# Attention with a bias on one core: three landing tiles for V, a smaller V ring, two spare E tiles, and three moves of V placed later

## The chip, the cores and the metric

The kernel runs on one core of one Trainium2 chip. The metric is the device time in microseconds (us) of one execution; lower is better. The same kernel is run several times, and the median counts.

## The reference: what is computed

```python
def setup_inputs():
    batch, n_heads, seq_len, head_dim = 4, 8, 1024, 64
    # q, k, v: (4, 8, 1024, 64) float32; bias: (1, 1, 1024, 1024) float32; all randn * 0.1

def reference(q, k, v, bias):
    scale = 1.0 / np.sqrt(head_dim)
    scores = scale * np.matmul(q, k.transpose(0, 1, 3, 2)) + bias
    scores_max = np.max(scores, axis=-1, keepdims=True)
    attn = np.exp(scores - scores_max) / (np.sum(np.exp(scores - scores_max), axis=-1, keepdims=True) + 1e-8)
    return np.matmul(attn, v).astype(np.float32)
```

So 32 heads of softmax attention, each of 1024 queries by 1024 keys, with one bias for all heads.

## The kernel before

**Tiling.** The 32 heads are taken as 16 pairs (pr), and the pairs in two groups of 7 and 9. One unit of work, a *slot*, is one chunk of 128 queries of one head against all 1024 keys: 256 slots. Scores live in three score places (`pl`, two PSUM banks each), and a slot belongs to place 0, 1 or 2. Scores are kept in a place from head to head: a fill adds to a place the difference between the next head's scores and the last one's (the arrays ke and qe hold this head's and the negated former head's halves), so the bias is put in only where a chunk starts in a place (`start`, L241), and every other fill is 8 matmuls of 128 x 128 (L244).

**A slot's way.** TensorE fills its place (L244). ScalarE takes the exponential into a bf16 tile E (`exp`, L258). TensorE multiplies E with V (`av`, L312), 8 matmuls into one of the 7 units of a PSUM bank `po`; a column of ones in V gives the row sum. When a bank has 7 units (or 6), VectorE evacuates it (`evac`: reciprocal L320, multiply L322 into `ob`), and stores go out on SP's queue; for the last two banks of the kernel they go out on ScalarE's queue (`close`, L679). There is no subtraction of the maximum.

**Slots on VectorE.** Twenty slots, all of place 2, take their exponential on VectorE instead (`d_steps`): a first step from the place into `dy` (L275), then df, dt, df, dt, de (L280 to L295). The first step sets place 2 free. Up to three such slots are open at a time, two of them in their later steps.

**Loads.** K, Q, V and bias come by DMA from GpSimd's queue (POOL), which turns float32 into bf16 on the way. POOL issues in order. From pair 7 on each load first waits, by a tiny copy (`tick`, L467), for the landing of the load but one before. K and Q are transposed by TensorE into `px` and copied out by VectorE (ko L199, qo L201), and further copies (ke, qe) are made by VectorE, or from pair 7 on by DMAs on SP's queue (L538). The late query chunks of pairs 0 and 1 are loads of their own (`qrest`). The loads stand early on POOL in this order: k1, q1, v0, k2, q2, k3, q3, v1, k4, q4, v2, k5, q5, v3, k6, q6, v4, v5, bias chunk 3, qrest of pairs 0 and 1, bias chunk 4, v6, bias chunks 5 to 7.

**V.** A pair's V lands in a tile of the pool `vland` (2 tiles), and a copy on VectorE (`move_v`, L492) moves it into the ring `vall` of VR = 24 heads, that is 12 pairs, where `av` reads it. So V of pair p may be moved only when all slots of pair p - 12 have been multiplied, and loaded only when V of pair p - 2 has left its landing tile.

**The order of the work** is fixed when the program is built. A planner inside the kernel (the loop at its end) keeps a clock for each engine with costs written by hand, and in each round lets the engine that can start first take its next piece: `pe_pick` for TensorE, `dve_pick` for VectorE (by ready time, then a priority), the oldest filled slot for ScalarE, the earliest ready DMA for SP. POOL gets a load when `next_v` or `load` issues it. On the chip every engine runs its list in order, and waits only where data or a buffer is missing. Whether a slot goes to VectorE is decided at its fill by `may_d` and an estimate of VectorE's `backlog`. The planner lets ScalarE write an E tile only when the slot NE = 13 exps earlier has been multiplied; the pool `ep` has as many tiles.

Of the kernel before, what the change touches and what calls it, by code (L numbers as in the profile page):

```python
# [16 lines left out]
def kernel(  # L17
# [31 lines left out]
    RING = 9  # L49
    LANDS = 5  # L50
    NE = 13
    C0 = 3

    consts = ctx.enter_context(tc.tile_pool(name="consts", bufs=1))
    land = ctx.enter_context(tc.tile_pool(name="land", bufs=LANDS))
    vland = ctx.enter_context(tc.tile_pool(name="vland", bufs=2))
    kq = ctx.enter_context(tc.tile_pool(name="kq", bufs=RING))
    ep = ctx.enter_context(tc.tile_pool(name="ep", bufs=NE))
    op = ctx.enter_context(tc.tile_pool(name="op", bufs=2))
    dp = ctx.enter_context(tc.tile_pool(name="dp", bufs=2))  # L60
    dy = ctx.enter_context(tc.tile_pool(name="dy", bufs=3))
# [15 lines left out]
    zeros = ep.tile([P, NCH, P], BF, name="E")[:, :4].rearrange("p c q -> p (c q)")  # L77
    braw = consts.tile([P, NCH, S], BF)

    VR = 24  # L80
    vall = consts.tile([P, VR, NCH, D1], BF)

    b0f = dp.tile([P, S], F32, name="df")
# [5 lines left out]
    slots = []  # L89
# [20 lines left out]
    NS = len(slots)  # L110
# [10 lines left out]
        at_place[x[0]] = s  # L121

    dslots = set()
    may_d = [x[0] == 2 and 36 < s < NS - 18 and not any(y[3] for y in slots[s:s + 4]) for s, x in enumerate(slots)]

    raws, lands, arrs = {}, {}, {}

# [205 lines left out]
    with tc.manual_schedule():  # L335
# [65 lines left out]
        v_at, vland_at = {}, {0: 13000}  # L401
        t_dma = 15900
        DUE = (64, 82, 94, 106, 117, 126, 134, 142, 150)
        t_pe, t_act, t_dve, t_pool = 9300.0, 9900.0, 9600.0, 9000
# [23 lines left out]
        dav = []  # L428
        dve_q = []
# [6 lines left out]
        free_lands, loads, loads_v = set(), list(range(EARLY, NP)), []  # L436
        sp_q, t_sp = [], T0
        AHEAD, SLACK = 60, 300
        DEP = 115
        ROOM = 5000  # L440
        MARGIN = 0
        WINDOW = 4

# [37 lines left out]
        def next_v(t):  # L481

            while loads_v and not any(x[2] // 2 == loads_v[0] - VR // 2 and y not in av_done for y, x in enumerate(slots)):
                if loads_v[0] - 2 not in v_at:
                    break
                p = loads_v.pop(0)
                vland_at[p] = issue(t, 1600, LATE, load_v, p)
                move_v(p)

        def move_v(pr):  # L490
            def run(t2):
                nc.vector.tensor_copy(vall[:, 2 * pr % VR:2 * pr % VR + 2, :, :D], lands[pr, "v"][:])  # L492
                v_at[pr] = t2 + 480 + L_DVE
                next_v(v_at[pr])
            dve_q.append((vland_at[pr], 0.3, 480, run))


        def early(kind, pr):
# [76 lines left out]
        def pe_cands():  # L575

            out = []
            for x in range(3):
                if not queue[x] or queue[x][0] > next_fill + WINDOW:
                    continue  # L580
                s = queue[x][0]
                r = fill_ready(s)
                if r is not None and (before[s] is None or before[s] in used):
                    cost = FILL + BIAS * bool(slots[s][3] and s > 1)

                    def do(t, s=s, x=x, cost=cost):
                        nonlocal next_fill
                        fill(s)
                        filled[s] = t + cost + L_PE
                        queue[x].pop(0)  # L590
                        next_fill = min([y[0] for y in queue.values() if y], default=NS)
                        if may_d[s] and backlog(t) < ROOM and len(open_d) < 3:
                            dslots.add(s)
                            avq.remove(s)
                            start_d(s)
                        else:
                            acts.append(s)
                    out.append((max(t_pe, r), cost, do, 0, s))
# [15 lines left out]
            if todo:  # L614
                r, group = min(todo)
# [4 lines left out]
                else:  # L620
                    f, tag = min((x_free[y], y) for y in x_free)
                    r = max(r, f)
# [19 lines left out]
            if pieces:  # L642
                pr, which, c0, n = pieces[0]
# [3 lines left out]
                if ((pr, which, c0) in raw_at and next_fill >= need - AHEAD and (ring < 0 or last_slot[ring] < next_fill)  # L647
                        and (lag < 4 or need - next_fill < 8)):
                    f, tag = min((x_free[y], y) for y in x_free)
                    r = max(f, raw_at[pr, which, c0])  # L650
# [40 lines left out]

        chains, d_wait, open_d = [], [], set()

        def backlog(t):
            x = max(0, t_dve - t) + sum(y[2] for y in dve_q if y[0] < t + 3000 and y[1] < 3)
            return x + sum(sum(y[0] for y in c) for c in chains) / 2 + sum(sum(y[0] for y in c[1:]) for r, s, c in d_wait) / 2

        def start_d(s):
            steps = d_steps(s)
            open_d.add(s)  # L700

            def first(t):
                steps[0][1]()
                used[s] = t + steps[0][0] + L_DVE
                d_wait.append((t + steps[0][0] + DEP, s, steps))
                next_chain(t)
            dve_q.append((filled[s], 0.5, steps[0][0], first))
# [46 lines left out]
            return min(ok + fills, key=lambda x: (x[0], x[3])) if ok + fills else None  # L754

        def dve_pick():
            can = [x for x in dve_q if x[1] < 4 or len(dav) < 2]
            if not can:
                return None
            best = min(can, key=lambda x: (max(x[0], t_dve), x[1]))  # L760
            start = max(best[0], t_dve)

            if best[1] >= 3:
                soon = [x for x in dve_q if x[1] < 3 and x[0] < start + 350]
                if soon:
                    best = min(soon, key=lambda x: (x[0], x[1]))
            return best
# [4 lines left out]
        while next_fill < NS or next_act < len(acts) or avq or dav or dve_q or sp_q:  # L772
            c = []
            if next_act < len(acts):

                s = min(x for x in acts[next_act:] if filled[x] <= max(t_act, filled[acts[next_act]]))
                acts.remove(s)
                acts.insert(next_act, s)
                if next_act < NE or acts[next_act - NE] in av_done:
                    r = max(t_act, filled[s], av_done[acts[next_act - NE]] if next_act >= NE else 0)  # L780
# [62 lines left out]
```

## Time and profile before

| what | value |
|---|---|
| median of 3 runs | 235.19 us (233.59 to 235.63) |
| the profiled execution | 235.16 us; its span, from the first to the last instruction, 233.4 us |
| granted TensorE clock | 0.997 |
| TensorE matmuls, busy | 222.3 us (95% of the span) |
| ScalarE, busy | 221.1 us (95%) |
| VectorE, busy | 201.5 us (86%) |
| GpSimd, busy | 63.4 us (27%) |
| exps on ScalarE (L258) | 237, 218.0 us busy, 1089 ns each |
| first steps on VectorE (L275) | 20, 1220 ns each |
| loads of V | 16 of 256 KB, median 6.1 us from issue to landing |

The profile shows one execution. Busy time of an engine is the union of its instructions, which may overlap. "Idle before, releaser" in a row is the time in which the engine had nothing running, and what ended it. Lines are named by their number in the kernel before (L312), tiles by their names in it (`po<-vall,E` writes po and reads vall and E).

### The profile page before, as it was taken

How to read it: one execution, taken by the hardware profiler on the slowest of the kernel's cores; microseconds unless marked ns; L12 is line 12 of the kernel's file. 1: busy time of each engine (PE TensorE's matmuls, PEld its weight loads, DVE VectorE, ACT ScalarE, POOL GpSimd, SP SyncE). 2: the span in 40 equal slices, each digit the busy share in tenths (PEclk: the TensorE clock that was granted, in tenths of full speed). 3: DMA queues.
4: the chain of work that ended last, by engine and by line, in shares of the span. 5: the costliest groups of instructions: out<-in, count | busy, mean ns of one | idle time of the engine just before them, and what ended most of it. 6: DMA issues, size and time to landing. Idle time of an engine off the chain costs nothing. (4 is left out here: it accounts for less than half of the span.)

```text
span 233.4 us, 10703 instructions
## 1 busy us (share of the span) xinstructions
PE 222.3 (95%) x4671; PEld 209.3 (90%) x4671; DVE 201.5 (86%) x296; ACT 221.1 (95%) x241; POOL 63.4 (27%) x99
## 2 busy tenths in 40 slices
PE   7989999899999999999999997999999999999992
PEld 2869999798999999999999997999999999999982
DVE  2576677599999998999999869999998999999972
ACT  3799999988999999999999998999999999999993
POOL 8943135055446555245352310000000000000000
PEclk9999999999999999999999999999999999999998
DMA  6999979959999899999999992111111111221212
GB/s 206 206 205 215 224 166 158 229 121 150 120 191 137 131 159 183 204 196 157 197 163 201 204 194 68 44 42 39 44 37 42 45 42 42 65 59 42 66 48 56
DMA packets 55646, 29.75 MB, mean 127 GB/s; under 512 B 31472, under 2 KB 51952, under 8 KB 55600
## 3 DMA queue, kind: packets, MB, share of 16 engines
q0 software_dynamic: 30336, 14.06, 48.7%
q1 hardware_dynamic: 24832, 14.40, 22.6%
q8 instruction: 36, 0.59, 1.1%
q10 hardware_dynamic: 432, 0.62, 0.8%
q14 instruction: 10, 0.08, 0.1%
HBM read 29.36 MB, written 8.39 MB: 162 GB/s over the span
## 5 line engine op out<-in xcount | busy, mean ns | idle before, releaser
L258 ACT ACTIVATE E<-pl 128x1024 bf16<-128x1024 f32 (+1 forms) x237 | 218.0, 1089 | 4.3 <-PE pl L244 3.9
L312 PE MATMUL po<-vall,E 128*128 128x65 bf16 x1888 | 93.6, 194 | 0.9 <-ACT E L258 0.9
L312 PEld LDWEIGHTS <-E 128*128 128x128 bf16 x1888 | 78.1, 98 | 1.9 <-ACT E L258 1.2
L244 PE MATMUL pl<-qo,ko 128*128 128x128 bf16 x1024 | 77.3, 219 | 1.7 <-DVE dy L275 1.1
L244 PEld LDWEIGHTS <-ko 128*128 128x128 bf16 x1160 | 69.2, 98 | 4.5 <-issue 1.5
L244 PE MATMUL pl<-qe,ke 128*128 128x128 bf16 x888 | 66.8, 219 | 1.9 <-DVE qe L212 0.5
L244 PEld LDWEIGHTS <-ke 128*128 128x128 bf16 x888 | 53.2, 98 | 5.0 <-issue 1.3
L275 DVE TENSOR_SCALAR dy<-pl 128x1024 int32<-128x1024 f32 x20 | 24.4, 1220 | 2.1 <-PE pl L244 1.4
L322 DVE TENSOR_TENSOR ob<-po,rs 128x448 f32<-128x448 f32 (+2 forms) x39 | 23.2, 594 | 1.9 <-DVE rs L320 0.5
L295 DVE SCALAR_TENSOR_TENSOR de<-dy,dt 128x1024 uint16<-128x1024 int32 x20 | 24.4, 1218 | 0.0
L290 DVE SCALAR_TENSOR_TENSOR dt<-df,dt 128x1024 f32<-128x1024 f32 x20 | 24.4, 1218 | 0.0
L284 DVE SCALAR_TENSOR_TENSOR dt<-df 128x1024 f32<-128x1024 f32 x20 | 24.3, 1217 | 0.0
L287 DVE SCALAR_TENSOR_TENSOR df<-dt,df 128x1024 f32<-128x1024 f32 x20 | 24.3, 1216 | 0.0
L199 DVE COPY ko<-px 128x1024 bf16<-128x1024 bf16 (+1 forms) x16 | 10.7, 671 | 6.9 <-PE px L191 6.3
L165 POOL DMA_DIRECT2D v<-in_v_dram x16 | 11.4, 712 | 18.3 <-DVE vall L492 16.0
L138 POOL DMA_DIRECT2D q<-in_q_dram x18 | 16.0, 890 | 1.3 <-DMA out_dram<-ob 0.5
L201 DVE TENSOR_SCALAR qo<-px,sgn 128x1024 bf16<-128x1024 bf16 (+2 forms) x18 | 12.4, 688 | 4.4 <-PE px L191 3.6
L280 DVE TENSOR_SCALAR df<-dy 128x1024 f32<-128x1024 uint16 x20 | 13.8, 690 | 0.0
L241 PE MATMUL pl<-ident,braw 128*128 128x128 bf16 x136 | 11.5, 228 | 0.1
L145 POOL DMA_DIRECT2D k<-in_k_dram x15 | 11.0, 734 | 2.2 <-PE pl L244 1.0
L320 DVE RECIPROCAL rs<-po 128x7 f32<-128x7 f32 (+3 forms) x40 | 7.8, 195 | 4.4 <-PE po L312 4.0
L467 POOL COPY tick<-q 1x1 bf16<-1x1 bf16 x9 | 3.8, 421 | 24.7 <-DMA q<-in_q_dram 24.7
(54 smaller groups left out, 129.5 us busy)
## 6 DMA issues: line engine op xcount, KB each, us to landing
v<-in_v_dram POOLq DMA_DIRECT2D x16, 256.0 KB, 6.1
k<-in_k_dram POOLq DMA_DIRECT2D x15, 256.0 KB, 5.6
out_dram<-ob SPq DMA_DIRECT2D x32, 96.0 KB, 3.6
out_dram<-ob SPq DMA_DIRECT2D x45, 64.0 KB, 3.2
ke<-ko SPq DMA_DIRECT2D x22, 128.0 KB, 4.9
q<-in_q_dram POOLq DMA_DIRECT2D x18, 128.0 KB, 4.8
qe<-q SPq DMA_DIRECT2D x17, 128.0 KB, 4.9
out_dram<-ob SPq DMA_DIRECT2D x67, 32.0 KB, 1.8
```

The costliest lines, as they stand in the source:

```text
L138: nc.gpsimd.dma_start(out=t[:, :, y, :], in_=(qf, kf)[x][pr][:, y].rearrange("p (c d) -> p c d", d=D))
L201: nc.vector.tensor_scalar(t["qo"][:, cs, :], px[:], sgn[:], None, op0=ALU.mult)
L244: nc.tensor.matmul(to, kk[:, kc, :], qq[:, c, :], start=False, stop=True, skip_group_check=True)
L258: nc.scalar.activation(e[:, i:i + n].rearrange("p b x -> p (b x)"), places[slots[s][0]][:, i:i + n].rearrange("p b x -> p (b x)"), ACTF.Ex ...
L275: w.tensor_scalar(t["y"][:], places[slots[s][0]].rearrange("p b x -> p (b x)"), scale * LOG2E * 65536.0, 127.0 * 65536.0, op0=ALU.mult, op ...
L280: w.tensor_scalar(t["f"][:], t["lo"], G / 65536.0, None, op0=ALU.mult)
L284: w.scalar_tensor_tensor(t["t"][:], t["f"][:], -G, t["f"][:], op0=ALU.add, op1=ALU.mult)
L287: w.scalar_tensor_tensor(t["f"][:], t["t"][:], Q, t["f"][:], op0=ALU.mult, op1=ALU.add)
L290: w.scalar_tensor_tensor(t["t"][:], t["f"][:], V, t["t"][:], op0=ALU.add, op1=ALU.mult)
L295: w.scalar_tensor_tensor(etile[s].bitcast(U16).rearrange("p c q -> p (c q)"), t["y"][:], 1.0 / 512.0, t["t"][:], op0=ALU.mult, op1=ALU.add)
L312: nc.tensor.matmul(po[:, j + i, :], etile[s][:, kc, :], vall[:, slots[s][2] % VR, kc, :], start=j + i + kc == 0, stop=kc == NCH - 1, skip_ ...
L322: nc.vector.tensor_tensor(ob[:, :n, :], po[:, :n, :D], rs[:, :n, :].to_broadcast([P, n, D]), op=ALU.mult)
```

## The change

- `vland` has 3 tiles instead of 2 (VL), and a load of V waits for the move of the V three pairs before instead of two.
- The ring `vall` holds 18 heads (9 pairs) instead of 24: V of pair p waits for the slots of pair p - 9.
- `ep` has 15 tiles; the planner goes on planning with 13.
- The slots that go to VectorE are given by a list, PLAN, in place of the estimate. The list holds the twenty slots that the estimate chose before.
- The limit of three open slots on VectorE is now kept when VectorE picks a first step, and no longer at the fill.
- The planner counts V of pairs 13 to 15 as landed 2.5 us later than it did, so their moves come later in VectorE's order.

Since the planner places everything, the order of the three parts follows: on POOL, V of pair 8 goes out ahead of K of pair 11, and V of pairs 9 to 15 all behind Q of pair 15 (before, V of pairs 8, 9 and 10 stood among the loads of K and Q). From there on VectorE's and TensorE's lists differ in places, with the same number of instructions of each kind but for the sizes of some evacuations. At the end, ScalarE's queue has five stores instead of two: the last bank but one holds six units instead of two.

```diff
--- before.py
+++ after.py
@@ -49,13 +49,16 @@
     RING = 9
     LANDS = 5
     NE = 13
+    VL = 3
+
+    SPARE = 2
     C0 = 3
 
     consts = ctx.enter_context(tc.tile_pool(name="consts", bufs=1))
     land = ctx.enter_context(tc.tile_pool(name="land", bufs=LANDS))
-    vland = ctx.enter_context(tc.tile_pool(name="vland", bufs=2))
+    vland = ctx.enter_context(tc.tile_pool(name="vland", bufs=VL))
     kq = ctx.enter_context(tc.tile_pool(name="kq", bufs=RING))
-    ep = ctx.enter_context(tc.tile_pool(name="ep", bufs=NE))
+    ep = ctx.enter_context(tc.tile_pool(name="ep", bufs=NE + SPARE))
     op = ctx.enter_context(tc.tile_pool(name="op", bufs=2))
     dp = ctx.enter_context(tc.tile_pool(name="dp", bufs=2))
     dy = ctx.enter_context(tc.tile_pool(name="dy", bufs=3))
@@ -77,7 +80,7 @@
     zeros = ep.tile([P, NCH, P], BF, name="E")[:, :4].rearrange("p c q -> p (c q)")
     braw = consts.tile([P, NCH, S], BF)
 
-    VR = 24
+    VR = 18
     vall = consts.tile([P, VR, NCH, D1], BF)
 
     b0f = dp.tile([P, S], F32, name="df")
@@ -121,9 +124,8 @@
         at_place[x[0]] = s
 
 
-
     dslots = set()
-    may_d = [x[0] == 2 and 36 < s < NS - 18 and not any(y[3] for y in slots[s:s + 4]) for s, x in enumerate(slots)]
+    PLAN = (38, 47, 50, 59, 75, 78, 96, 108, 117, 129, 150, 159, 171, 177, 189, 195, 207, 216, 225, 234)
 
     raws, lands, arrs = {}, {}, {}
 
@@ -437,7 +439,6 @@
         sp_q, t_sp = [], T0
         AHEAD, SLACK = 60, 300
         DEP = 115
-        ROOM = 5000
         MARGIN = 0
         WINDOW = 4
 
@@ -481,7 +482,7 @@
         def next_v(t):
 
             while loads_v and not any(x[2] // 2 == loads_v[0] - VR // 2 and y not in av_done for y, x in enumerate(slots)):
-                if loads_v[0] - 2 not in v_at:
+                if loads_v[0] - VL not in v_at:
                     break
                 p = loads_v.pop(0)
                 vland_at[p] = issue(t, 1600, LATE, load_v, p)
@@ -492,7 +493,7 @@
                 nc.vector.tensor_copy(vall[:, 2 * pr % VR:2 * pr % VR + 2, :, :D], lands[pr, "v"][:])
                 v_at[pr] = t2 + 480 + L_DVE
                 next_v(v_at[pr])
-            dve_q.append((vland_at[pr], 0.3, 480, run))
+            dve_q.append((vland_at[pr] + 2500 * (pr > 12), 0.3, 480, run))
 
 
         def early(kind, pr):
@@ -589,7 +590,7 @@
                         filled[s] = t + cost + L_PE
                         queue[x].pop(0)
                         next_fill = min([y[0] for y in queue.values() if y], default=NS)
-                        if may_d[s] and backlog(t) < ROOM and len(open_d) < 3:
+                        if s in PLAN:
                             dslots.add(s)
                             avq.remove(s)
                             start_d(s)
@@ -691,15 +692,10 @@
 
         chains, d_wait, open_d = [], [], set()
 
-        def backlog(t):
-            x = max(0, t_dve - t) + sum(y[2] for y in dve_q if y[0] < t + 3000 and y[1] < 3)
-            return x + sum(sum(y[0] for y in c) for c in chains) / 2 + sum(sum(y[0] for y in c[1:]) for r, s, c in d_wait) / 2
-
         def start_d(s):
             steps = d_steps(s)
-            open_d.add(s)
-
             def first(t):
+                open_d.add(s)
                 steps[0][1]()
                 used[s] = t + steps[0][0] + L_DVE
                 d_wait.append((t + steps[0][0] + DEP, s, steps))
@@ -754,14 +750,15 @@
             return min(ok + fills, key=lambda x: (x[0], x[3])) if ok + fills else None
 
         def dve_pick():
-            can = [x for x in dve_q if x[1] < 4 or len(dav) < 2]
+
+            can = [x for x in dve_q if (x[1] < 4 or len(dav) < 2) and (x[1] != 0.5 or len(open_d) < 3)]
             if not can:
                 return None
             best = min(can, key=lambda x: (max(x[0], t_dve), x[1]))
             start = max(best[0], t_dve)
 
             if best[1] >= 3:
-                soon = [x for x in dve_q if x[1] < 3 and x[0] < start + 350]
+                soon = [x for x in can if x[1] < 3 and x[0] < start + 350]
                 if soon:
                     best = min(soon, key=lambda x: (x[0], x[1]))
             return best
```

## The prediction

> **What bounds the kernel now.** I read the page first: ScalarE (ACT) and TensorE (PE) are busy 95% of the span, VectorE (DVE) 86%, GpSimd (POOL) 27%. One group holds ACT: 237 exps, 1089 ns each. They overlap: the last unbroken run of them is 94 in 86.31 us, so the pitch is (86.31 - 1.09) / 93 = 0.916 us, and the 237 alone need 217 of the 233.4 us. What can still be won is where that pitch breaks. The windows of the span show where:
>
> ```profile
> 40.00:50.00 10.00, 9.22 (x196) 8.81 (x194) 6.91 (x14) 9.10 (x11) 0.63 (x1) 1.00 1.02 203
> 50.00:60.00 10.00, 9.59 (x206) 9.11 (x202) 9.86 (x13) 9.41 (x11) 6.92 (x11) 1.00 1.01 119
> 140.00:150.00 10.00, 8.70 (x193) 8.33 (x190) 9.84 (x15) 9.13 (x11) 0.00 (x0) 1.00 0.23 64
> ```
>
> The columns after the length are PE, its weight loads, DVE, ACT, POOL, clock, DMA share and GB/s. ACT stands at 9.9 to 10.0 nearly everywhere else, at full clock. ACT's timeline names the holes (those under 0.2 us are not marked; windows of 2 us show idle of 0.10 in 42 to 44 and 0.13 in 44 to 46):
>
> ```profile
> 47.53 1.02 ACT L258 ACTIVATE E<-pl 128x1024 bf16<-128x1024 f32 x1 [0.26 <-PE pl L244]
> 55.28 17.52 ACT L258 ACTIVATE E<-pl 128x1024 bf16<-128x1024 f32 x19 [0.59 <-PE pl L244]
> 73.14 69.23 ACT L258 ACTIVATE E<-pl 128x1024 bf16<-128x1024 f32 x75 [0.34 <-PE pl L244]
> 143.24 86.31 ACT L258 ACTIVATE E<-pl 128x1024 bf16<-128x1024 f32 x94 [0.87 <-PE pl L244]
> ```
>
> An idle time of g costs ACT g + (1.09 - 0.92) = g + 0.17 us, since the overlap is lost too. Always it is PE's fill that came late. PE's timeline says why:
>
> ```profile
> 42.11 0.47 PE L191 MATMUL px<-ident,qrest 128*64 128x128 bf16 x10 [0.78 <-DMA qrest<-in_q_dram]
> ...
> 54.13 0.61 PE L244 MATMUL pl<-qe,ke 128*128 128x128 bf16 x8 [0.36 <-DVE dy L275]
> ...
> 142.59 0.61 PE L244 MATMUL pl<-qo,ko 128*128 128x128 bf16 x8 [1.14 <-DVE dy L275]
> ```
>
> So a late load of q, and twice a late first step (dy) of a DVE head, which holds score place 2. DVE was late because it had waited itself:
>
> ```profile
> 42.62 0.55 DVE L201 TENSOR_SCALAR qo<-px,sgn 128x640 bf16<-128x640 bf16 x1 [1.88 <-PE px L191]
> ...
> 46.96 0.43 DVE L492 COPY vall<-v 128x1024 bf16<-128x1024 bf16 x1 [0.85 <-DMA v<-in_v_dram]
> ...
> 138.33 0.43 DVE L492 COPY vall<-v 128x1024 bf16<-128x1024 bf16 x1 [1.86 <-DMA v<-in_v_dram]
> ```
>
> And the early loads are late because POOL's queue, which issues in order, stood behind two landing tiles of V:
>
> ```profile
> 20.70 0.71 POOL L165 DMA_DIRECT2D v<-in_v_dram  x1 [3.79 <-DVE vall L492]
> ...
> 27.20 0.70 POOL L165 DMA_DIRECT2D v<-in_v_dram  x1 [4.39 <-DVE vall L492]
> ...
> 32.77 0.74 POOL L165 DMA_DIRECT2D v<-in_v_dram  x1 [4.88 <-DVE vall L492]
> ...
> 34.05 1.42 POOL L155 DMA_DIRECT2D qrest<-in_q_dram  x2
> ```
>
> **The change, part by part.** In the order of instructions, PE and DVE are the same up to about 85 us (V8's move is the first that shifts); the counts of every kind stay, and the twenty DVE heads of PLAN are those of before, with the same six steps each. So the sum is of waits, not of work.
>
> *Third landing tile, early part.* The loads at 27.20 and 32.77 are V4 and V5; they waited for the moves of V2 (26.48 to 26.89) and V3. With three tiles V5 waits for V2's move only, so V5, bias chunk 3 and both qrest go out 32.77 - 27.20 = 5.6 us sooner, qrest at 28.5. The two qrest took 8.0 and 8.6 us to land, so 37.1; even with the 10.9 us of the slowest V load 39.4, ahead of the 41.3 at which PE wants it. V6 waits for V3's move (ends 32.5): at 10.9 us it lands at 43.4, and DVE now comes to its move at 46.96 - 0.85 - 0.78 = 45.3. PE's wait of 0.78 and DVE's of 0.78 and 0.85 go. On ACT the two small holes vanish, 0.10 + 0.17 and 0.13 + 0.17, together 0.57; and the dy of 52.86, which made PE late at 54.13, can come 1.6 us sooner, more than the 0.36 that PE waited: 0.59 + 0.17 = 0.76. Gain 1.33 (bounds 0.57 and 1.33). The three holes at 47 to 50 (0.26, 0.21, 0.21) I leave: there PE runs bias and score fills of some 1.2 us each without idling. Loads pulled forward meet the copies of ke that SP issues at 29.83 and 36.34; of 22 such copies the quickest landed in 3.3 us, the slowest in 7.7. The first has its reader after 40 us, so even 7.7 is hidden behind some 3 us of slack: nothing in the sum.
>
> The Trainium skill (DMA: Bandwidth & Descriptors, "Issuing engines are not separate DMA queues") speaks against pulling loads forward: what POOL and SP issue runs on the same 16 DMA engines and interleaves. The spread from 3.3 to 7.7 us of equal copies agrees. By that rule only the DMA idle time ahead of qrest can be won; the windows show a DMA share of 0.37 at 32 to 34, some 1.3 us, and qrest would land at 42.1 - 1.3 = 40.8, still ahead of PE; the sum would be the same with 0.5 us of slack.
>
> *V13 to V15 later, VL 3 at 130 to 140 us.* By places in DVE's order the moves of V9 to V15 now stand where DVE of before stood at 124.0, 127.8, 129.5, 134.0, 137, 141 and 148.6 us, in place of 101 to 141. The move that waited 1.86 (V14: issued 131.15, landed 7.2 later) now stands some 3 us later and behind the dy that PE waited for. PE's 1.14 and ACT's 0.87 go: 0.87 + 0.17 = 1.04 (bounds 0 and 1.04).
>
> *Ring of 18.* The loads of V9 to V15 now wait for pairs 0 to 6, not 0 to 3 for the last four, and so stand on POOL behind the last q load. Before, the V loads at 82.52, 92.02 and 109.85 stood between k11 (77.35) and the V load at 120.70; the first now goes ahead of k11, the other two behind q15. Each of the two cost its issue of 0.70, a tick of 0.51, and 6.4 / 5 = 1.3 us of waiting for its landing. So V9 goes out 2.4 to 5.0 us sooner, at 115.7 to 118.3. V loads there landed in 5.0 to 7.2 us: 120.7 to 125.5 against 124.0. V10 and V11 follow at 3.5 us each (the loads at 124.89 and 128.38 did) and need to land by 127.8 and 129.5. Most of that is in time, and I take no wait; the late end is a rival. V15's move also needs the last reader of pair 6 (slot 108), which PE's order places several exps ahead of it. The shorter memset of vall (218 ns before) lies in the start-up wait for DMA.
>
> *Two spare E tiles; open heads counted at their first step.* No row has ACT waiting for an attention matmul (po), so nothing is gained; no reason for a loss.
>
> *The tail.* The order moves one thing that costs. The bank before the last held 2 units and one store on ACT's queue, then the last store (olast). Now it holds 6 units and four stores, all on ACT's queue ahead of olast. Evacuating 6 takes 0.20 + 0.56 where 2 took 0.17 + 0.29: ready at 229.95, not 229.65. Stores issue at 0.38 (ACT, one row) to 0.47 us (SP, back to back), so olast goes out at 231.5 to 231.85 in place of 230.53. Five SP stores, which had ended together with olast (the last issued at 230.73), are now out earlier, so ACT decides. Against 230.73 that is 0.8 to 1.1 us; I take 1.05, as SP's rows are the nearer kind.
>
> Sum: 0.57 + 0.76 + 1.04 - 1.05 = 1.32 us less. The profiled execution took 235.16 us (span 233.4, 1.8 around it), the median of the runs is 235.19. 235.16 - 1.32 = **233.8 us**, 0.6% less.
>
> **Rivals.**
> 1. *The early lead carries on, or the tail is hidden.* PE, freed of 0.78 us, enters the bias stretch ahead and the three holes go (0.43 + 0.38 + 0.38), as does that at 73.14 (0.51): 233.8 - 1.7 = 232.1. If instead the four stores cost nothing, 232.8. For it: PE has idle to give. Against: only three score places, so PE can't run far ahead.
> 2. *The early loads are bound by DMA, not by POOL's wait.* The 1.33 is not won: 235.2. For: the DMA share is about 1 from 34 to 48 us. Against: 0.37 at 32 to 34.
> 3. *The ring starves DVE at V9 to V11 (slower).* If q15 goes no sooner, V9 is issued at 120.7, V10 at 124.9, V11 at 128.4, landing at 125.7, 129.9 and 133.4 at best against 124.0, 127.8, 129.5: DVE waits up to 3.9 us. The 1.86 us of before cost ACT 1.04, so 2.2, and in proportion to a 7.2 us landing 3.4. With the early gain, the tail and 1.04 not won but replaced: 235.16 - 1.33 + 1.05 + 2.2 = 237.1. It decides if V9 is issued after 124.0 - 5.0 = 119.0. For: all seven stand in one row behind q15. Against: two loads fewer ahead of it.
>
> **How the numbers follow.** The forecast 0.50, rival 1 0.22, rival 2 0.10, rival 3 0.18. One per cent, 2.35 us, is about what a measurement of this kernel can tell from no change. The forecast lies within it but near enough that 0.13 of its 0.50 goes over; rival 1 is faster; rival 2 is the same; rival 3 is slower but for 0.01. Faster 0.13 + 0.22 = 0.35; same 0.37 + 0.10 + 0.01 = 0.48; slower 0.18 - 0.01 = 0.17. The range reaches down past rival 1 to 231.8 and up to 236.9, into rival 3. The forecast's own range is 232.9 (tail at 0.1) to 234.9 (V14's wait only replaced).
>
> **What would show it.** Right: no wait for qrest on PE; POOL's waits for V moves before 40 us shrink from 16.0 us; no DVE wait above 0.5 for a V load; ACT without holes at 55 and 142; the last store of ACT issued about 2.1 us after the last exp's end, not 1.0. Wrong: DVE waiting for V at 124 to 131 us, or new holes of ACT after 85 us where the order differs.

## The result and the profile after

The changed kernel takes 235.41 us (median of 20 runs, 234.44 to 236.33), the kernel before 233.63 us in the same comparison (20 runs, 232.87 to 235.94): ratio 1.0055, 95% interval 1.0035 to 1.0075. So it is slower by 0.6%, where 0.6% faster was forecast; the time lies in the stated range. The prediction held one per cent to be what a measurement of this kernel can tell from no change; with 20 runs on each side the interval is 0.2% either way, and the change of 0.55% stands clear of it.

One number on the side of before has to be set right first. The forecast started from 235.16 us, the profiled execution, which agreed with the median of the three runs shown. Over 20 runs the median is 233.63: the profiled execution was one of its longer ones, by 1.5 us. The profiled execution of after took 236.30 us, 0.9 above its median.

The page of after, span and busy times:

```profile
span 234.5 us, 10684 instructions
...
PE 221.6 (95%) x4671; PEld 209.1 (89%) x4671; DVE 202.1 (86%) x296; ACT 221.1 (94%) x241; POOL 62.8 (27%) x99
```

The counts of instructions are those that the change promised, and the work is the same. The windows of the span that the prediction showed of before, now of after (columns as there):

```profile
40.00:50.00 10.00, 9.31 (x196) 8.83 (x193) 7.63 (x16) 9.09 (x10) 3.63 (x7) 1.00 1.05 168
50.00:60.00 10.00, 9.83 (x205) 9.47 (x203) 9.86 (x12) 9.43 (x11) 3.55 (x8) 1.00 1.06 126
140.00:150.00 10.00, 9.95 (x226) 9.81 (x223) 9.41 (x15) 10.00 (x12) 0.00 (x0) 1.00 0.29 81
```

From 140 to 150 us ACT went from 9.13 to 10.00. In the two early stretches it stands where it stood (9.10 and 9.41 before), though 1.33 us were to be won there. ACT's timeline:

```profile
44.10 4.04 ACT L260 ACTIVATE E<-pl 128x1024 bf16<-128x1024 f32 x4 [0.33 <-PE pl L246]
...
55.90 17.52 ACT L260 ACTIVATE E<-pl 128x1024 bf16<-128x1024 f32 x19 [0.36 <-PE pl L246]
73.76 155.12 ACT L260 ACTIVATE E<-pl 128x1024 bf16<-128x1024 f32 x169 [0.34 <-PE pl L246]
229.31 1.79 ACTq L689 DMA_DIRECT2D out_dram<-ob  x4
231.48 0.34 ACTq L689 DMA_DIRECT2D out_dram<-olast  x1
```

The hole at 142 is gone: 169 exps run without a break to 228.88, against 229.55 before, so the exps ended 0.67 us sooner. But a new hole stands at 44, that of 55 is only smaller (0.36 for 0.59), and the row of stores behind the last exp is long. ACT's timeline of before had this there, with the last exp ended at 229.55:

```profile
229.68 0.38 ACTq L688 DMA_DIRECT2D out_dram<-ob  x1
230.53 0.34 ACTq L688 DMA_DIRECT2D out_dram<-olast  x1
```

From the end of the last exp to the end of the span before took 3.84 us and after 5.62: 1.78 us more, which alone is the difference of the two medians (235.41 - 233.63 = 1.78).

The early loads came as forecast. POOL of after:

```profile
27.40 0.71 POOL L167 DMA_DIRECT2D v<-in_v_dram  x1 [4.92 <-DVE vall L493]
...
28.64 1.42 POOL L157 DMA_DIRECT2D qrest<-in_q_dram  x2
...
32.98 0.75 POOL L167 DMA_DIRECT2D v<-in_v_dram  x1 [2.37 <-DVE vall L493]
```

The first qrest, issued at 28.64, landed at 37.50. PE no longer waits for it, and waits all the same:

```profile
36.68 0.59 PE L314 MATMUL po<-vall,E 128*128 128x65 bf16 x13 [0.48 <-issue]
42.10 0.25 PE L193 MATMUL px<-ident,qrest 128*64 128x128 bf16 x2
43.04 0.41 PE L193 MATMUL px<-ident,qrest 128*64 128x128 bf16 x8 [0.69 <-issue]
```

"Issue" means that no semaphore, no DMA of data and no other engine held the instruction. The ten transposes of qrest, one row of ten in before, are broken after the second. DVE, behind PE, waits longer at the same two places (1.94 and 1.90 us, where before waited 0.89 and 1.88), but no longer for a V load:

```profile
39.03 0.75 DVE L203 TENSOR_SCALAR qo<-px,sgn 128x1024 bf16<-128x1024 bf16 x1 [1.94 <-PE px L193]
43.50 0.55 DVE L203 TENSOR_SCALAR qo<-px,sgn 128x640 bf16<-128x640 bf16 x1 [1.90 <-PE px L193]
...
137.42 0.42 DVE L493 COPY vall<-v 128x1024 bf16<-128x1024 bf16 x1
141.48 0.42 DVE L493 COPY vall<-v 128x1024 bf16<-128x1024 bf16 x1
```

### The profile page after: what moved, and what is told of

The parts are those of the page before. It is cut to its first block, busy times and chain, and to the rows that moved or that the text cites. A ratio compares the mean times of both kernels' runs of the same rounds, so it can differ in the third digit from the quotient of the medians.

```text
span 234.5 us, 10684 instructions
## 1 busy us (share of the span) xinstructions
PE 221.6 (95%) x4671; PEld 209.1 (89%) x4671; DVE 202.1 (86%) x296; ACT 221.1 (94%) x241; POOL 62.8 (27%) x99
## 4 chain that ended last, share of the span: by engine, by line
PE 48%; ACT 31%; issue 11%; DMA 4%; POOL 3%; DVE 2%; ACTq 0%; POOLq 0%; DVEq 0%
ACT E L260 31%; PE pl L246 28%; PE po L314 14%; DMA q<-in_q_dram 4%; PE px L193 3%; PE pl L243 3%; DVE dy L277 1%; POOL k L147 1%; PE px L189 1%; POOL braw L162 1%; DVE dt L292 0%; POOL qz L352 0%; POOL qs L353 0%; POOL v L167 0%; POOL q L157 0%
## 5 line engine op out<-in xcount | busy, mean ns | idle before, releaser
L324 DVE TENSOR_TENSOR ob<-po,rs 128x448 f32<-128x448 f32 (+1 forms) x39 | 23.2, 594 | 1.5
L286 DVE SCALAR_TENSOR_TENSOR dt<-df 128x1024 f32<-128x1024 f32 x20 | 24.4, 1218 | 0.0
L297 DVE SCALAR_TENSOR_TENSOR de<-dy,dt 128x1024 uint16<-128x1024 int32 x20 | 24.4, 1218 | 0.0
L140 POOL DMA_DIRECT2D q<-in_q_dram x18 | 16.7, 931 | 4.5 <-DVE ob L324 2.8
L282 DVE TENSOR_SCALAR df<-dy 128x1024 f32<-128x1024 uint16 x20 | 14.3, 717 | 0.0
L322 DVE RECIPROCAL rs<-po 128x7 f32<-128x7 f32 (+2 forms) x40 | 7.8, 196 | 6.0 <-PE po L314 5.4
L468 POOL COPY tick<-q 1x1 bf16<-1x1 bf16 x9 | 5.6, 627 | 27.0 <-DMA q<-in_q_dram 27.0
```

The lines of the kernel that those rows point to most:

```text
L140: nc.gpsimd.dma_start(out=t[:, :, y, :], in_=(qf, kf)[x][pr][:, y].rearrange("p (c d) -> p c d", d=D))
L282: w.tensor_scalar(t["f"][:], t["lo"], G / 65536.0, None, op0=ALU.mult)
L286: w.scalar_tensor_tensor(t["t"][:], t["f"][:], -G, t["f"][:], op0=ALU.add, op1=ALU.mult)
L297: w.scalar_tensor_tensor(etile[s].bitcast(U16).rearrange("p c q -> p (c q)"), t["y"][:], 1.0 / 512.0, t["t"][:], op0=ALU.mult, op1=ALU.add)
L324: nc.vector.tensor_tensor(ob[:, :n, :], po[:, :n, :D], rs[:, :n, :].to_broadcast([P, n, D]), op=ALU.mult)
```

## What lies beneath the wait: TensorE's own instructions

The page has a queue that the prediction passed over:

```profile
q8 instruction: 36, 0.59, 1.1%
```

The 36 transfers make up 0.59 MB, 16 KB each. PE has 9,342 matmuls and weight loads, with its semaphore and drain instructions 9,379; over 36 that is a little more than 256. So these look like PE's program, fetched in blocks while it runs. Three readings of the traces support it. First, PE's breaks by "issue" lie at fixed counts: in after the instructions that come late are PE's number 1,218 and 1,474, which is 256 apart; in all eight traces with a break at the transposes of qrest (after, e1, e2, e4, e6, e10, e11, e12) it is number 1,474; later breaks (e1 at 97.22, e3 at 102.18, e11 at 96.40 and 103.00 us) are at 3,778 and 4,034, that is 1,474 plus nine and ten times 256. In the fourteen traces no other idle time above 0.2 us ahead of a matmul is put down to "issue". At each of these breaks the number of the late instruction is 256 times the transfers that had ended, plus 194: 4 had ended at number 1,218, and 5, 14 and 15 at the others. Second, PE resumes 1.3 to 1.6 us after a transfer of this queue ended: in after at 35.25 (resumed 36.68) and 41.61 (resumed 43.04). Third, with a transfer that ended sooner there is no break (38.06 in e7, below, 39.73 in e8, 39.83 in e3).

By the same count, with a block from each number 256 n + 194 to the next, one can ask how long after PE's entry into one block the transfer of the next had ended. From 145 us on, where the DMA share in windows of before and after is 0.13 to 0.21, it was 0.8 to 2.4 us (182 transfers of all traces, median 1.5). For the transfer that decides the break at 42 us it was 3.6 to 5.5 us in all traces but e7 (2.6), beside a block of some 5.5 us. Where it was above 4.6 us PE shows the break, with one exception, the profiled execution of before (4.63).

The Trainium skill (Runtime: NRT & Kernel Launch, "Instruction fetch mechanics") says that an engine's sequencer fetches its program in 16 KiB blocks of 256 instructions over a DMA queue of its own while it executes the current one, and that the cost of a block's end is mostly hidden. The blocks agree with the counts here; that the cost is hidden does not hold in these stretches, where the breaks were 0.25 to 1.35 us long.

In the profiled execution of before the same transfer had ended at 40.47. PE could have gone on at about 40.47 + 1.43 = 41.90, and the wait for qrest ended at 42.11. Two waits ended within 0.2 us of each other, and the profile named the one that came last: by this estimate some 0.6 of the 0.78 us would have stayed without the wait for qrest.

## The experiments

Two questions were put: what does the tail cost by itself, and why did the early gain not come? The theories for the second are that TensorE's own instructions come late (in the expectations of the first eight kernels this is Theory 2), or that something else of the new order eats the gain. Where an expectation numbers its theories, it states them itself. Each ratio is to the kernel before as it ran beside that kernel on the same chip; its median there was 234.47 us for e1 to e4, 233.69 for e5 to e8 and 234.09 for e9 to e12.

To compare stages over executions, I take from each trace the starts of ACT's 237 exps and sum, over a stage, how far each start lies behind the one before it beyond 0.906 us, about the undisturbed pitch. The result is ACT's loss in that stage, in us:

| execution | 30 to 60 us | 60 to 120 | 120 to 150 | 150 to the end | last exp's end to span's end |
|---|---|---|---|---|---|
| before | 2.65 | 1.29 | 1.59 | 0.66 | 3.84 |
| e5, before again | 1.70 | 1.30 | 0.56 | 0.68 | 3.86 |
| e9, before with more stores on ACT | 1.71 | 1.30 | 1.48 | 0.67 | 3.79 |
| e4, before with qrest first | 2.32 | 1.28 | 0.56 | 0.67 | 3.85 |
| e6, e4 with room for the fetch | 2.89 | 1.29 | 0.54 | 0.69 | 3.84 |
| e8, before with V13 to V15 delayed | 1.71 | 1.28 | 0.53 | 0.76 | 4.61 |
| after | 3.14 | 1.08 | 0.49 | 0.85 | 5.62 |
| e10, after again | 1.91 | 1.07 | 0.49 | 0.85 | 5.63 |
| e2, after without spare E | 1.98 | 1.36 | 0.36 | 0.84 | 5.59 |
| e1, after with split tail | 2.04 | 1.58 | 0.49 | 0.84 | 3.99 |
| e11, the same again | 1.97 | 2.34 | 0.49 | 0.85 | 4.01 |
| e12, after, olast on SP | 2.05 | 1.17 | 0.39 | 0.85 | 4.44 |
| e7, after with split tail and room for the fetch | 1.51 | 1.23 | 0.38 | 0.85 | 4.02 |
| e3, after, early V in 2 tiles | 1.68 | 1.46 | 1.79 | 1.11 | 5.61 |

The last two columns repeat to within 0.1 us for the same instructions. The first three are partly chance.

### e1 and e11: the tail taken apart

```diff
-                for to, of_ in evac(b):
-                    w = nc.scalar if last else nc.sync
-                    sp_q.append((t2 + cost + L_DVE, lambda t3, to=to, of_=of_: w.dma_start(out=to, in_=of_), last))
+                for n, (to, of_) in enumerate(evac(b)):
+                    w = nc.scalar if last and (len(units) == 1 or n % 2) else nc.sync
+                    sp_q.append((t2 + cost + L_DVE, lambda t3, to=to, of_=of_, w=w: w.dma_start(out=to, in_=of_), last))
```

> The changed kernel, with the four stores of the last bank but one shared out: every other one goes on SP's queue, the rest and olast on ScalarE's. Nothing else moves. Theory 1 (the five stores in one row on ScalarE's queue cost the tail some 1.6 us): the last store is issued about 1.0 to 1.4 us after the last exp's end and not 2.6, and the time falls by 1.2 to 1.6 us against the changed kernel, so to about 0.999 to 1.001 of the kernel before. Rival (the tail is set by what follows the stores, the landing and the closing of the program, and the store order is hidden): the time stays at 1.0055 of before, within 0.002.

Measured: 0.9975 of before (0.9946 to 1.0003), 233.79 us. The timeline of its end, all engines but PE:

```profile
228.48 0.56 DVE L324 TENSOR_TENSOR ob<-po,rs 128x384 f32<-128x384 f32 x1
229.06 0.81 SPq L689 DMA_DIRECT2D out_dram<-ob  x2
229.07 0.85 ACTq L689 DMA_DIRECT2D out_dram<-ob  x2
...
230.01 0.40 ACTq L689 DMA_DIRECT2D out_dram<-olast  x1
```

Two queues take two stores each, and olast goes out 1.37 us after the last exp's end (228.64) instead of 2.60. The tail is 3.99 us, 1.63 less than after's. Everything else of the change is still in, so without the tail the change is worth between nothing and 0.5%. It was run once more on the chip of the last four kernels:

> The kernel after with the four stores of the last bank but one taken in turn by SP and ScalarE, once more, against the kernel after on the same chip. Theory 1: 1.6 to 1.9 us below the kernel after; against before a ratio of 0.996 to 1.000, because what is left of the change (third landing tile, later moves) takes away waits that before has only in some of its executions. Rival (the change without its tail is worth the 2.4 us that the prediction gave it): ratio 0.990 to 0.993.

Measured: 233.97 us, 0.9994 of before (0.9966 to 1.0022), and 1.73 us below the kernel after on that chip (235.70). The 2.4 us that the prediction gave to the rest of the change would be a ratio of 0.990; both intervals exclude it.

### e10: the kernel after once more

No edit.

> The kernel after once more, for a second profile of it and on the same chip as the others of this call. Theory 1: ratio 1.004 to 1.007; tail 5.6 us again (it is the same instructions each time), while the early excess of ScalarE, 30 to 60 us, is another than the 3.1 us of its first profile, anywhere from 1.5 to 3. Rival (the early excess belongs to the new order): again 2.9 to 3.3 us there.

Measured: 235.70 us, 1.0077 (1.0049 to 1.0105). Its tail is 5.63 us, its loss from 30 to 60 us 1.91 where the first profile of after had 3.14. PE still has its break at the same instruction, 0.33 us long. So the long tail belongs to the kernel, and 1.2 us of the early loss in the first profile belonged to that execution.

### e12: only the last store moved

```diff
-                    w = nc.scalar if last else nc.sync
+                    w = nc.scalar if last and len(units) > 1 else nc.sync
```

> The kernel after, with the four stores of the last bank but one left on ScalarE's queue and only the very last store (olast) on SP's. Theory 1 (the price is the last store's place behind four others): olast goes out within 0.1 us of its data, about 1.0 us after the last exp's end, and the fourth ob store, issued some 1.8 us after it, ends the span: tail 4.6 to 4.8 us instead of 5.6, ratio 1.001 to 1.003. Rival (four stores in one queue and their landing set the end, whatever the last one does): tail 5.4 to 5.6, ratio 1.005 to 1.006.

Measured: 234.60 us, 1.0021 (0.9995 to 1.0047). The timeline of its end:

```profile
227.72 1.80 ACTq L689 DMA_DIRECT2D out_dram<-ob  x4
...
228.02 0.23 DVE L324 TENSOR_TENSOR olast<-po,rs 128x64 f32<-128x64 f32 x1
228.27 0.33 SPq L689 DMA_DIRECT2D out_dram<-olast  x1
```

olast leaves 0.02 us after its data (228.02 + 0.23), and the four stores of the bank are still in one row. The tail is 4.44 us, 1.18 below after's. So most of the price is the last store's place behind four others, and the rest is the row of four itself.

### e9: the same number of stores on the side of before

```diff
             last = len(av_done) >= NS - 1
+            late = len(av_done) >= NS - 3
...
-                for to, of_ in evac(b):
-                    w = nc.scalar if last else nc.sync
-                    sp_q.append((t2 + cost + L_DVE, lambda t3, to=to, of_=of_: w.dma_start(out=to, in_=of_), last))
+                for n, (to, of_) in enumerate(evac(b)):
+                    act = last or late and n > 1
+                    w = nc.scalar if act else nc.sync
+                    sp_q.append((t2 + cost + L_DVE, lambda t3, to=to, of_=of_, w=w: w.dma_start(out=to, in_=of_), act))
```

> The kernel before, except that three of the five stores of its last full bank go out on ScalarE's queue behind the last exp, so that four stores stand ahead of the last one there, as in the kernel after. Theory 1 (in a usual execution the two kernels differ by the tail alone, and the tail's price is the row of stores ahead of the last): from the end of the last exp to the end of the span 5.1 us instead of 3.84 (three stores of 0.45 us more ahead of olast, less nothing), time 1.2 to 1.7 us above before, ratio 1.005 to 1.007. Rival (what makes the kernel after slower lies in its new order, and its long tail is only where the lost time shows): ratio 1.000 to 1.002.

Measured: 233.73 us, 0.9998 (0.9968 to 1.0028), tail 3.79. My expectation missed by the whole 1.2 us. ACT's timeline says why:

```profile
142.91 86.32 ACT L258 ACTIVATE E<-pl 128x1024 bf16<-128x1024 f32 x94 [0.51 <-PE pl L244]
228.62 1.85 ACTq L689 DMA_DIRECT2D out_dram<-ob  x4
230.56 0.39 ACTq L689 DMA_DIRECT2D out_dram<-olast  x1
```

ACT issues the row of four from 228.62, while its last exp is still running (it ends at 142.91 + 86.32 = 229.23). The row ends at 230.47, and olast's data were ready only at 230.18. So olast left 0.38 us late, which cost nothing, since in before a store of SP, landed 2.87 us after the last exp's end, had the last word, and here olast itself, landed 2.83 us after it. Five stores on ACT's queue are therefore not the price by themselves. The price is the row together with the time at which its data are ready: in before the bank of seven is evacuated 0.65 us ahead of the last exp's end, in after the bank of six 0.40 us behind it (228.72 + 0.56 against 228.88). The banks are cut otherwise by the new order (six and one, where before had seven, two and one); that this cut is what put the row late follows from these times, and no run changed the cut alone.

### e2: no spare E tiles

```diff
-    SPARE = 2
+    SPARE = 0
```

> The changed kernel with no spare E tiles (13 instead of 15); the order on every engine is the same. Theory: ScalarE never waited for an E tile, so the time is that of the changed kernel, 1.0055 of before within 0.002, and the idle times of ScalarE in the profile are the same within 0.3 us in sum. Rival (the spare tiles take part in the result: they save waits behind late attention matmuls): 0.5 us or more slower than the changed kernel, so 1.008 or more.

Measured: 235.72 us, 1.0067 (1.0036 to 1.0098), beside 1.0055 and 1.0077 of after. The two tiles are worth nothing that can be measured.

### e3: the early V loads back in two tiles

After with SPARE = 0, where V of pairs 0 to 6 (EARLY = 7) lands in a pool of two tiles of its own, and later V in three:

```diff
+    vland2 = ctx.enter_context(tc.tile_pool(name="vland2", bufs=2))
...
-        lands[pr, "v"] = vland.tile([P, 2, NCH, D], BF, name="v16")
+        lands[pr, "v"] = (vland2 if pr < EARLY else vland).tile([P, 2, NCH, D], BF, name="v16")
```

> The changed kernel, no spare E tiles, and V of pairs 0 to 6 again in two landing tiles of their own (V of pairs 7 to 15 in three others); the order on every engine is the same, so only the early waits of POOL come back. Theory 2 (the earlier loads win nothing, since TensorE's instructions, which come over the same DMA engines, arrive later beside them): the waits of TensorE named issue at 36.2 and 42.4 us are gone or under 0.2 us, the wait for qrest of 0.8 us at 41 to 42 us is back, and the time is that of the run without spare tiles or up to 0.6 us less. Rival (the earlier loads do bring 1.3 us and something else takes it back): 1.0 us or more slower than the run without spare tiles.

Measured: 235.18 us, 1.0031 (0.9999 to 1.0063). DVE's timeline:

```profile
126.30 0.43 DVE L494 COPY vall<-v 128x1024 bf16<-128x1024 bf16 x1 [1.37 <-DMA v<-in_v_dram]
...
131.70 0.43 DVE L494 COPY vall<-v 128x1024 bf16<-128x1024 bf16 x1 [0.83 <-DMA v<-in_v_dram]
...
142.72 0.43 DVE L494 COPY vall<-v 128x1024 bf16<-128x1024 bf16 x1 [0.86 <-DMA v<-in_v_dram]
```

Early it behaves like before (loss 1.68, no break at qrest, transfer of PE's instructions ended at 39.83). But V9 now goes out at 119.15, beyond the 119.0 that the prediction's third rival named as its point, and DVE starves at V9 and V11 as that rival said, and at V14 too (the three rows); ACT loses 1.79 from 120 to 150 us. This profiled execution took 236.76 us, 1.6 above the median of e3, so a usual one may lose less. In after V9 went out at 111.53. So the early third tile has one real effect: it keeps POOL some 5 us ahead (the first K load behind the bias is issued at 44.90 in after, at 49.65 in e3 and 50.41 in before), and that lead is what the smaller ring lives on. In time e3 is not told from after.

### e4: before, with qrest ahead

Before, with the two qrest loads moved ahead of V5 and bias chunk 3, and the planner's due times of these loads held at their old values, so that the order on every other engine stays:

```diff
-        ... "v3", "k6", "q6", "v4", "v5", "b3", "q0", "q1", "b4", ...
+        ... "v3", "k6", "q6", "v4", "q0", "q1", "v5", "b3", "b4", ...
```

> The kernel before, with one thing changed on POOL: the two loads of qrest go out behind V of pair 4, ahead of V of pair 5 and bias chunk 3. The order on all other engines is that of before. The loads then land 4 us or more ahead of the transposes that read them, so TensorE's wait of 0.78 us for them must go. Theory 2 (beneath that wait lay one for TensorE's own instructions): an idle time of TensorE named issue stands at the same transposes, ending 1.4 us after a DMA of 16 KB on the instruction queue, and the time is that of before within 0.3 us. Rival (the load was the only thing that was late): no such idle time, and 0.5 to 1.3 us faster than before, a ratio of 0.994 to 0.998.

Measured: 234.30 us, 0.9980 (0.9952 to 1.0009). qrest landed at 34.69, 7 us ahead of need. PE's timeline:

```profile
41.13 0.25 PE L191 MATMUL px<-ident,qrest 128*64 128x128 bf16 x2
42.21 0.41 PE L191 MATMUL px<-ident,qrest 128*64 128x128 bf16 x8 [0.83 <-issue]
```

With its data there for 7 us PE still stands, after the second transpose, until 1.40 us after the transfer of its instructions (40.80). So the load alone was not what had to be won. Moving it had a price as well: only the order of loads on POOL differs from before, PE enters the block from number 962 at 30.2 us (30.3 in before), and the transfer of the next block ended 3.76 us after that, in before 1.84.

### e6 and e7: room for the fetch

e6 is e4 with a tick ahead of each of bias chunks 5 to 7, so that fewer loads are in flight at 40 us; e7 is e1 with the same tick ahead of chunks 4 to 7:

```diff
+                if pr >= 5:
+                    nc.gpsimd.tensor_copy(tick[:], flight[-2][0])
```

> The run with qrest first, and also bias chunks 5, 6 and 7 held back on POOL: each first waits by a tiny copy for the landing of the load but one before it. The order on all other engines is that of the kernel before. Theory 2 (TensorE's instructions arrive late because their DMA of 16 KB stands beside a long row of loads): the DMA on the instruction queue near 40 us ends by about 40.1 us, TensorE's idle time at the transposes of qrest falls under 0.3 us (it was 0.82), and the time is 0.3 to 0.9 us under that of the run with qrest first, a ratio of 0.993 to 0.997 of before. Rival (the moment of that DMA is set by TensorE's own progress alone): it ends at 40.5 to 40.9 as before, the idle time stays at 0.6 to 0.9 us, the time at 0.998.

Measured for e6: 234.75 us, 1.0047 (1.0019 to 1.0075), slower by half a per cent. The transfer ended at 41.73, later than in e4, and PE's break is the longest seen:

```profile
43.23 0.41 PE L191 MATMUL px<-ident,qrest 128*64 128x128 bf16 x8 [1.35 <-issue]
```

> The changed kernel with the last stores shared out between SP and ScalarE, and bias chunks 4 to 7 held back on POOL by a tiny copy each. The order on TensorE and VectorE is that of the changed kernel. Theory 2: no idle time of TensorE named issue above 0.3 us between 30 and 50 us, and 0.3 to 1.0 us less than with the shared stores alone, a ratio of 0.993 to 0.996 of before. Rival: as with the shared stores alone, 0.9975, with 0.4 to 0.7 us of idle at the transposes of qrest.

Measured for e7: 233.83 us, 0.9999 (0.9964 to 1.0034). In its trace the transfer ended at 38.06, there is no break, and the loss from 30 to 60 us is 1.51, the least of all; its median does not show it. The ticks of e6 did not help, those of e7, one more and against another order, went with an early fetch in one execution. How to give the fetch room stays open.

### e5: before once more

No edit.

> The kernel before once more, unchanged, for a second trace. Theory 3 (the loss of ScalarE at 142 us isn't in every execution: V of pair 14 landed 7.2 us after its issue in the first trace and 5.3 us in the run with qrest first, which has the same order there): the landing of V14 differs from 138.3 us by 1 us or more, and VectorE's wait for it is under 1.0 us. Rival (it is in every execution of this order): a wait of 1.5 us or more for V14 and an idle time of ScalarE of 0.8 us or more at 142 to 144 us. In either case an idle time of TensorE of 0.6 to 0.9 us at the first transposes of qrest, which ends with the load or 1.4 us after the instruction DMA, whichever is later.

Measured: 233.66 us in one run; the median of before on that chip is 233.69. ACT's timeline, and then PE's:

```profile
50.00 22.28 ACT L258 ACTIVATE E<-pl 128x1024 bf16<-128x1024 f32 x24 [0.20 <-PE pl L244]
72.62 155.40 ACT L258 ACTIVATE E<-pl 128x1024 bf16<-128x1024 f32 x169 [0.34 <-PE pl L244]
```

```profile
41.77 0.59 PE L191 MATMUL px<-ident,qrest 128*64 128x128 bf16 x10
```

Neither the wait for qrest, nor the hole at 55, nor the hole at 142 is there. All three terms that the change was to win were absent in this execution of the kernel before, whose time is the usual one. The first qrest took 6.1 us to land instead of 8.0, V14 5.7 instead of 7.2.

### e8: the delay of V13 to V15 alone

```diff
-            dve_q.append((vland_at[pr], 0.3, 480, run))
+            dve_q.append((vland_at[pr] + 2500 * (pr > 12), 0.3, 480, run))
```

> The kernel before with one line of the change alone: the planner counts V of pairs 13 to 15 as landed 2.5 us later. Landing tiles, ring and E tiles are those of before. The last two banks then hold one unit each, with one store each on ScalarE's queue. Theory 3 (the wait for V14 goes; it costs 1.0 us in some executions and little in others, 0.5 us in the mean; the tail is that of before or better): no wait of VectorE for V above 0.5 us after 130 us, and a ratio of 0.996 to 0.999. Rival (the forecast's term, 1.04 us in every execution): 0.994 to 0.996. Against both: if two landing tiles make the later moves hold up V15's load, VectorE waits 1 us or more for V15 and the ratio is above 1.000.

Measured: 234.16 us, 1.0018 (0.9997 to 1.0040). Its loss from 120 to 150 us is 0.53, as in e5. Its end came out differently again: two stores from the one tile olast, the second evacuation waiting 1.25 us for the first store, tail 4.61 us. The delay's gain cannot be told from this pair of times.

## Why the prediction was wrong, point by point

**The sign.** Gains of 2.37 us were to outweigh a tail of 1.05. The gains came to nothing early and some 0.1 to 0.5 us at V14, and the tail to 1.78: the terms follow one by one.

**The base.** Each term was priced from one execution that turned out to be 1.5 us above the median, and the terms were the losses that made it so. The note that it agreed with the median of three runs gave false comfort. That the measured time lies in the range is luck in part: with the median of 20 runs as base the same sum gives 233.63 - 1.32 = 232.3, and the range, shifted by the same 1.5 us, would end at 235.4, where the measured time lies.

**Early part, -1.33.** The step that failed is "PE's wait of 0.78 goes". The loads behaved as worked out (V5 issued at 27.40 for 27.2, qrest at 28.64 for 28.5 and landed at 37.50 for 37.1; POOL's waits for V moves between 18 and 40 us down from 3.79 + 4.39 + 4.88 to 4.92 + 2.37 us), but beneath the wait lay the fetch of PE's own instructions; e4 shows a break of 0.83 us there on the kernel before, with qrest long landed. The 16.0 us that the prediction gave to POOL's waits before 40 us are those of the whole span; 15.0 lie before 40. Over the loss from 30 to 60 us the usual value is 1.7 in before's order (e5, e8 and e9; 2.65 in the first trace) and about 2.0 in after's (six of seven traces between 1.5 and 2.1): nothing won, perhaps 0.3 lost.

The prediction priced loads pulled forward at nothing for what else moves by DMA, and that is the second error of this step: the transfer one block earlier ended at 32.2 to 33.0 us in the five executions with the old timing of these loads (before, e3, e5, e8, e9), and at 33.9 to 35.3 in the nine with qrest issued at 27.7 to 29.2. PE enters the block ahead at 30.0 to 31.1 us in all fourteen, so it is not PE that came later: from that entry it is 1.8 to 2.1 us in the five and 3.7 to 4.7 in the nine. e4 against before moves these loads forward and e3 against e2 moves them back, and each lands in the other group, so the loads pulled forward delay the fetch. That they do it by sharing the DMA engines is the likely way, and was not tested by itself. No old-timed trace shows a break at the transposes of qrest, and eight of the nine others do. Rival 2, that the early loads are bound by DMA, was right that nothing is won and wrong on the transfer: data came in time, instructions did not. That its 235.2 lies near the measured 235.41 is luck too, since it stands on the same base.

**V14's wait, -1.04.** The mechanism was right and its frequency was wrong. The loss from 120 to 150 us is about 1.5 in two of five executions in before's order (before, where V14's move waited 1.86 us, and e9, where V15's waited 1.22; not e4, e5, e6) and 0.36 to 0.49 in all seven in after's with the early third tile. Against 0.56 the usual gain is 0.1 to 0.2 us; over all executions, with two in five, about 0.5.

**Ring of 18, no cost.** Right: V9 left at 111.53 and no V load was waited for. That the third rival's mechanism is real e3 showed, at the very point that was named, though in a long execution.

**Spare E, no cost.** Right (e2).

**Tail, +1.05.** Right in kind, too small by 0.7: 5.62 - 3.84 = 1.78, the same within 0.05 in every trace of these ends. By time, after lies 1.73 above e11 on one chip, where the tails differ by 1.62 in the traces. The row of four took 1.79 us as priced. What was not priced: ACT then let 0.38 us pass before olast (231.10 to 231.48), olast took 1.93 us to land instead of 1.72, and the term was counted against SP's last store (issued at 230.73) and not olast's (230.53).

Put together against a usual execution of before (e10 against e5): +0.21 from 30 to 60, -0.23 to 120, -0.07 to 150, +0.17 to the end, +1.77 tail, in sum 1.85 us; the medians say 1.78 and, on the last chip, 1.61. Of the signs named in advance, "no wait for qrest", "no DVE wait for V" and "ACT without a hole at 142" came true; the hole at 55 stayed, and the last store went out 2.60 us after the last exp's end, not 2.1.

No kernel tried is shown to be better than before. e1 and e11 (0.9975 and 0.9994) are the best of after's kind.

## What to carry to other kernels

Price a wait by what would hold the instruction next, and look for the engine's own instruction fetch among the candidates: a break with the releaser "issue", always at the same instruction count, is its sign. Before a hole of half a microsecond is counted as gain, look whether a second execution has it: the holes behind V loads and qrest came and went here with landings that differed by up to 2 us between executions of the same instructions. A row of stores at the end is counted from when its data are ready against the last instruction of the engine that issues them, not by its length: five stores on ACT's queue cost nothing in e9, and the end of after, with as many, is 1.78 us longer.

## What the hardware showed that was not expected

- TensorE ran out of instructions: with 256 per transfer, it resumed 1.3 to 1.6 us after the transfer's end, with breaks of 0.25 to 1.35 us, most of them at 42 us, where the DMA share of the windows is about 1, in three executions also near 100 us.
- The transfer of TensorE's next block had ended 0.8 to 2.4 us after TensorE entered the block before it, from 145 us on, and up to 5.5 us after it at 36 to 42 us (e6).
- ACT issues stores while an exp is still executing (e9: from 228.62, the exp ended at 229.23).
- Stores of one queue in an unbroken row at the end go out 0.38 to 0.54 us apart, on ACT's as on SP's queue.
